# A two-layer attention and MLP trunk: another order of instructions, compressed scores inside a longer run, and an MLP without row factors

## The chip, the cores and the metric

The kernel runs on one core of a Trainium2 chip. The metric is the device time of one execution in microseconds. Engines are named as the profile names them: TensorE (PE, its weight loads PEld), VectorE (DVE), ScalarE (ACT), GpSimd (POOL) and SyncE (SP), whose queue issues the DMA transfers.

## What is computed

256 tokens of width 1024 pass through two layers. Each layer is a hybrid attention with a post-norm, and a squared-ReLU MLP of width 4096 with a post-norm, both around a residual:

```python
for l in range(DEPTH):
    h = _rms_norm(x, g_pre_mix[l])
    parts = jnp.split(h @ w_in[l], split_at, axis=-1)
    ...
    o_nsa = _nsa_mixer(...)      # 8 heads, 2 key heads: compressed, selected and window branch, gated
    o_fox = _fox_mixer(...)      # 8 heads, causal softmax with cumulative forget gates
    mix = jnp.concatenate([o_nsa, o_fox], axis=-1) @ w_out[l]
    x = x + _rms_norm(mix, g_post_mix[l])
    h = _rms_norm(x, g_pre_mlp[l])
    y = jnp.square(jax.nn.relu(h @ w_up[l])) @ w_down[l]
    x = x + _rms_norm(y, g_post_mlp[l])
```

`_rms_norm` divides by the root of the mean square plus 1e-6 and multiplies by a gain. In the compressed branch, keys and values of 32 tokens at a stride of 16 are flattened, pass a small two-layer network with gelu, and give 15 compressed keys and values for each key head. Queries are scored against them, the softmax of these scores (`pc`) weighs the compressed values, and it would also choose blocks of 64 tokens; as there are only four blocks and sixteen may be chosen, all of them are.

## The kernel before, in words

**Precision.** The large products are made from operands split in two parts of the type fp32r. For each chunk of weights ScalarE copies a rounded part `whi`, VectorE subtracts it to get `wlo` (`Weights.get`), and TensorE makes three products, hi·hi, lo·hi and hi·lo (`mm3`). The smaller products of attention, and the transposes, work on float32 operands directly. The tokens lie in two tiles of 128 (`NT`, index `t`).

**Stages.** For each layer: products of the normalised input with `w_in` in chunks (`in_chunk`; "c3", "c4" and so on are named groups of this filling work), attention, the output projection with `w_out`, norm and residual (`sandwich`), then `up` and `down` of the MLP in eight parts, norm and residual again. At the end of layer 0, `sandwich` makes the transposed input `xT` of layer 1, and layer 1's first products of `w_in` follow.

**What sets the order.** No instruction is issued where its line stands. The code runs against a `Recorder`, which notes every operation with its tiles, and `emit` issues them at line 392, the line that the profile shows for every instruction. Between the two stands a planner:

- `schedule` is a list scheduler. It keeps a time for each engine, and lets each engine take the ready operation with the lowest rank, as far as buffers are free. TensorE's rank is the recorded place (`key`), with the filling products in a lane of their own that runs at 0.9 of the main line's pace (`LANE`). A change of tile size on TensorE costs it `RETILE`, 145 ns.
- `order` runs it once with the recorded places, then calls `deadlines`, which works back from TensorE's order to a due time for each operation of the other engines, and runs `schedule` again with these due times as ranks, `PASSES` times. The last round counts.
- `_cost` and `_latency` give the planner's durations and delays. For TensorE, an fp32r product is taken as the larger of 107 ns and 3 + n/2.4 ns, a float32 product as the larger of 214 and n/0.6, transposes as 56 and 107 ns.
- `with nc.stretch()` binds several TensorE operations together, so that nothing gets between them.

So the planner's times decide what each of the five queues holds and in which order, and the chip then runs these queues with their semaphores.

**The places that the change touches.**

- *Compressed scores.* `hidden_part` makes the first product of the small network for keys ("k") and values ("v"): a stretch of 16 products on narrow tiles (`tile_position`, 32 columns of the array each, four side by side), named `o<-w,kst...` in the trace. `compressed_scores` scores the queries against the compressed keys (`kbd`) in a stretch of its own of four such products, `s<-qT,kbd`, and copies the result to `csT`. `compressed_exp` transposes it, adds the mask and takes the exponential; `compressed_scale` divides and makes `pcs`; `compressed_T` transposes it to `pcT`. `hidden_T` and `hidden_gelu` finish the values' network, `compressed_v` and `compressed_vT` give the block values `vbig`.
- *The attention loop.* A loop over 24 score tiles (16 of the sparse heads, 8 of the forgetting heads) calls for each `scores`, one step later `scale`, two steps later `probs_T` (three transposes of the softmax `pr`), and three steps later, for every second pair of heads, `pv` (a stretch of products on 64-wide tiles, `o<-pr...,v...`). Between them `fill(1)` puts in products of the next weights. The table `side` says beside which step each part of the compressed branch stands.
- *Block values.* After `pv` of sparse heads, one product of `vbig` and `pcT` adds the compressed branch to the same sum `o`. Its flags close the sum (`stop=True`). Then `o_evac` copies `o` to `oT`, split in two parts by ScalarE and VectorE.
- *Row factors of the MLP.* The input of the MLP is not divided by its root mean square. Because relu and square are homogeneous, the output only wants the factor r² per row. `row_factors` works out r, r² and r⁴ for each token tile, and `sandwich` takes them: `times` multiplies the sum by r² (a per-row scalar) and the gain in one `scalar_tensor_tensor`, and `rsqrt_sum` works out the root of r⁴·sum + eps.

Of the kernel before, what the change touches and what calls it, by code (L numbers as in the profile page):

```python
# [170 lines left out]
class Recorder:  # L171
# [103 lines left out]
    def order(self):  # L275

        for op in self.ops:
            op.rank = op.key
        out = self.schedule()
        for _ in range(PASSES):  # L280
            self.deadlines(out)
            out = self.schedule()
        return out

    def schedule(self):
# [41 lines left out]
        while events:  # L327
# [5 lines left out]
            for e, ops in waiting.items():  # L333
                while busy[e] <= t:
# [21 lines left out]
                    if e == "sync":  # L356
                        busy[e] = t + 450
                        bus = max(bus, t + 1150) + best.cost
                        best.end = bus + 900
                    else:  # L360
                        busy[e] = best.end = t + best.cost
                        if e == "tensor" and best.tile != tiled:
                            tiled = best.tile
                            busy[e] = best.end = best.end + RETILE
                    count += 1
# [55 lines left out]


def _cost(op, views):

# [5 lines left out]
    if op.engine == "tensor":  # L430
        if op.name == "stretch":

            return sum(x[1][0].ix.size / (2.4 if x[1][1].dtype == F32R else 0.6) + 20
                       for x in op.args[2]) / (P // min(op.tile))
        if op.name == "transpose":
            return 56.0 if op.args[1].dtype == F32R else 107.0
        if op.args[1].dtype == F32R:
            return max(107.0, 3 + n / 2.4)
        return max(214.0, n / 0.6)
    if op.engine == "vector":  # L440
# [63 lines left out]
def trunk(nc, A, consts_in, out, sbp, pp):  # L504
# [144 lines left out]

    def rsqrt_sum(a, b, factor=None):  # L650


        w = small([P, 6], "rsqrt", 6)
        c, d, h, y, t, r = (w[:, i:i + 1] for i in range(6))
        f = 1.0 if factor is None else factor
        nc.vector.tensor_scalar(c, a, f, EPS, op0=OP.mult, op1=OP.add)
        nc.vector.tensor_scalar(d, c, -0.5, None, op0=OP.mult)
        if factor is None:
            h = -0.5
        else:  # L660
            nc.vector.tensor_scalar(h, factor, -0.5, None, op0=OP.mult)
# [7 lines left out]
    def rstd_of_x(t, tag):  # L669
# [4 lines left out]
        return rsqrt_sum(ssq[:, 0:1], ssq[:, 1:2])  # L674

# [21 lines left out]

    def sandwich(t, acc, g_post, pre=None, xT=None, r4=None, r2=None, store=None):

# [4 lines left out]
        def times(name, n, gain):  # L704
            y = tokt(name)
            if r2 is None:
                nc.vector.tensor_mul(y, acc[n], gain[:, half(n)])
            else:
                nc.vector.scalar_tensor_tensor(y, acc[n], r2, gain[:, half(n)], op0=OP.mult, op1=OP.mult)
            return y  # L710

        for n in range(2):
# [4 lines left out]
            if n == 0 and not pre:  # L717
                m[0] = times("m", 0, g_post)
        r = rsqrt_sum(sq[:, 0:1], sq[:, 1:2], r4)
        if not pre:  # L720
# [54 lines left out]
    for l in range(DEPTH):  # L775
# [105 lines left out]
        def hidden_part(s, q):  # L881
            if q == 0:
                T["w1"] = []
            T["w1"].append(weight(l, "w1" + s, q))
            if q == 3:
                T["hid"] = psum("o")
                with nc.stretch():
                    for i in range(16):
                        c = i % 4
                        nc.tensor.matmul(T["hid"][32 * c:32 * c + 32, :256],  # L890
                                         kst[s][:, i, :, :].rearrange("p g n -> p (g n)"), T["w1"][i // 4][:, c, :],
                                         start=i < 4, stop=i >= 12, tile_position=(0, 32 * c))
                T["hs" + s] = tile([P, 256], F32, name="hs", tag="cum")
                nc.vector.tensor_copy(T["hs" + s], T["hid"][:, :256])
# [323 lines left out]

        def pv(o, pairs, last):


            with nc.stretch():
                for q, terms in enumerate(pairs):
                    for i, (pT, V, cols) in enumerate(terms):
                        for kb in range(2):
                            for par in range(2):
                                h = slice(par * HD, par * HD + HD)
                                c = cols[par]
                                if kb == 0:
                                    nc.tensor.matmul(o[h, q * S:q * S + S], V[0][:, c:c + HD], pT[par][:, 0:S],  # L1230
                                                     start=q == 0 and i == 0, stop=False, skip_group_check=True)
                                else:
                                    nc.tensor.matmul(o[h, q * S + P:q * S + S], V[1][:, c:c + HD], pT[par][:, S:S + P],
                                                     start=False, stop=last and i == len(terms) - 1,
                                                     skip_group_check=True)
# [10 lines left out]
        if first:  # L1246
            for n, _ in enumerate(in_chunk(0, evac0)):
                if n == 11:
# [4 lines left out]
                    for t in range(NT):  # L1253
                        r_mix[t] = rstd_of_x(t, "rm")
        else:

            for n, _ in enumerate(in_chunk(0, evac0, by_token=True)):
                if n == 6:
                    urgent(carry)
                    next(carry)  # L1260
                    for t in range(NT):
                        r_mix[t] = rstd_of_x(t, "rm")
        row_scales()
# [35 lines left out]
        for t in range(NT):  # L1299
# [14 lines left out]
        for i in range(len(flat) + 4):  # L1314
# [62 lines left out]
        r2s, r4s = [], []  # L1377
# [79 lines left out]
        for fc in range(8):  # L1457
# [25 lines left out]
            steps = [sandwich(t, [ys[t, 0], ys[t, 1]], g_post2, pre, xT, r4s[t], r2s[t],  # L1483
                              out[0].rearrange("(t p) d -> t p d", p=P)[t] if last_l else None) for t in range(NT)]
# [59 lines left out]
```

## Time and profile before

| what | value |
|---|---|
| time, median of 3 runs | 626.17 us (625.88 to 626.36) |
| the profiled execution's own time | 626.18 us |
| its span in the trace | 624.4 us |
| granted clock of TensorE | 0.998 |
| bytes moved | 115.70 MB, 185 GB/s |

Busy shares in 40 slices of 15.6 us, in tenths (9 is 90% or more):

```profile
PE   9999999999999999999999999999999999999995
DVE  6878999989986557566698899997997666566544
ACT  7757777577665455555566657764776555455432
DMA  8987446218766556654346883422396566556001
```

The first ten slices are layer 0's attention, the next ten its MLP; the twenty after them are the same for layer 1. TensorE is nearly always busy. VectorE is close to full in attention (slices 3 to 8, and 22 to 28) and half free in the MLPs; DMA is full only at the very start. In the rows that follow, a tile's name stands for all its buffers, `a<-b,c` is an output and its inputs, and since every instruction has line L392, groups are told apart by these names.

### The profile page before, as it was taken

The page shows a single profiled execution, that of the slowest core. Times are in us where ns is not written, and L with a number is a line of the kernel's source. Part 1 is how long each engine was busy: PE and PEld are TensorE (multiplying, and loading weights), DVE is VectorE, ACT ScalarE, POOL GpSimd, SP SyncE. Part 2 cuts the span into 40 slices and gives each one's busy share as a digit, 9 for nine tenths or more (in the row PEclk, how much of TensorE's full clock was granted, in tenths as well). Part 3 has the DMA queues.
Part 4 walks back from the last instruction along what each step waited for, and adds up shares of the span by engine and source line. Part 5 has one row for each costly group of instructions (what it writes and reads, how often), then busy time and mean ns, then how long its engine had stood idle before and what let it go on. Part 6 is the DMA issues. An engine that isn't in the chain of part 4 may idle for free.

```text
span 624.4 us, 9952 instructions
## 1 busy us (share of the span) xinstructions
PE 615.1 (99%) x3572; PEld 517.5 (83%) x3572; DVE 481.0 (77%) x1077; ACT 378.4 (61%) x736; POOL 0.2 (0%) x4
## 2 busy tenths in 40 slices
PE   9999999999999999999999999999999999999995
PEld 6988986788888888888888989778888888888884
DVE  6878999989986557566698899997997666566544
ACT  7757777577665455555566657764776555455432
POOL 0000000000000000000000000000000000000000
PEclk9999999999999999999999999999999999999999
DMA  8987446218766556654346883422396566556001
GB/s 322 403 341 257 150 153 199 88 56 318 266 192 203 194 175 201 198 180 136 102 156 218 303 290 118 164 81 90 105 318 204 183 186 209 180 189 193 22 1 68
DMA packets 33601, 115.70 MB, mean 185 GB/s; under 512 B 3984, under 2 KB 4112, under 8 KB 33552
## 3 DMA queue, kind: packets, MB, share of 16 engines
q1 hardware_dynamic: 33552, 115.07, 55.2%
q8 instruction: 28, 0.46, 0.3%
q14 instruction: 21, 0.17, 0.1%
HBM read 114.00 MB, written 1.05 MB: 184 GB/s over the span
## 4 chain that ended last, share of the span: by engine, by line
PE 91%; DVE 4%; DMA 2%; ACT 1%; issue 1%; DVEq 0%; SPq 0%
PE s L392 34%; PE acc L392 28%; PE x L392 24%; PE o L392 6%; DVE pr L392 2%; DMA wraw<-in_w_in_dram 1%; DVE wlo L392 1%; DMA first<-in_first_dram 1%; ACT whi L392 1%; ACT rl L392 0%; DVE cum L392 0%; DVE prT L392 0%; DVE st L392 0%; DVE prX L392 0%; ACT xT L392 0%
## 5 line engine op out<-in xcount | busy, mean ns | idle before, releaser
L392 DVE TENSOR_TENSOR wlo<-wraw,whi 128x1024 fp32r<-128x1024 f32 (+1 forms) x188 | 224.9, 1202 | 86.3 <-ACT whi L392 85.7
L392 ACT ACTIVATE whi<-wraw 128x1024 fp32r<-128x1024 f32 (+1 forms) x188 | 195.5, 1044 | 134.0 <-PE acc L392 70.3
L392 PE MATMUL s<-xT,whi 128*128 128x512 f32 x448 | 112.0, 392 | 0.0
L392 PEld LDWEIGHTS s<-xT,whi 128*128 128x128 f32 x448 | 81.4, 189 | 15.2
L392 PE MATMUL acc<-whi,aT 128*128 128x512 f32 x256 | 88.6, 390 | 0.0
L392 PE MATMUL x<-whi,aT 128*128 128x512 f32 x256 | 88.4, 390 | 0.0
L392 PEld LDWEIGHTS s<-xT,wlo 128*128 128x128 f32 x448 | 61.1, 190 | 4.4
L392 PE MATMUL s<-xT,wlo 128*128 128x256 f32 x448 | 62.5, 282 | 0.0
L392 PEld LDWEIGHTS acc<-whi,aT 128*128 128x128 f32 x256 | 48.0, 188 | 9.9
L392 PEld LDWEIGHTS x<-whi,aT 128*128 128x128 f32 x256 | 48.1, 188 | 9.6
L392 ACT ACTIVATE pr<-pr,st 128x256 f32<-128x256 f32 (+1 forms) x96 | 42.9, 450 | 15.6 <-DVE st L392 14.3
L392 PE MATMUL x<-wlo,aT 128*128 128x512 f32 x128 | 50.0, 390 | 0.0
L392 PE MATMUL acc<-wlo,aT 128*128 128x512 f32 x128 | 49.9, 390 | 0.0
L392 PE MATMUL acc<-xT,whi 128*128 128x256 f32 x256 | 48.8, 286 | 0.0
L392 PEld LDWEIGHTS acc<-xT,whi 128*128 128x128 f32 x256 | 40.4, 190 | 2.2 <-issue 1.2
L392 PE MATMUL x<-whi,xT 128*128 128x512 f32 x112 | 36.8, 400 | 0.4 <-ACT xT L392 0.3
L392 PE MATMUL acc<-xT,wlo 128*128 128x256 f32 x128 | 36.4, 285 | 0.0
L392 PE MATMUL acc<-whi,xT 128*128 128x512 f32 (+1 forms) x128 | 36.0, 352 | 0.0
L392 ACT ACTIVATE rl<-h 128x512 f32<-128x512 f32 x28 | 17.6, 629 | 18.2 <-DVE h L392 18.2
L392 PEld LDWEIGHTS acc<-wlo,aT 128*128 128x128 f32 x128 | 24.0, 188 | 5.0
L392 PEld LDWEIGHTS x<-wlo,aT 128*128 128x128 f32 x128 | 24.1, 188 | 4.5
L392 ACT ACTIVATE rl<-x 128x512 f32<-128x512 f32 x24 | 14.7, 612 | 21.6 <-PE x L392 16.6
(231 smaller groups left out, 974.7 us busy)
## 6 DMA issues: line engine op xcount, KB each, us to landing
wraw<-in_w_up_dram SPq DMA_DIRECT2D x64, 512.0 KB, 3.8
wraw<-in_w_down_dram SPq DMA_DIRECT2D x64, 512.0 KB, 3.6
wraw<-in_w_in_dram SPq DMA_DIRECT2D x36, 512.0 KB, 4.7
wraw<-in_w_out_dram SPq DMA_DIRECT2D x16, 512.0 KB, 6.2
w<-in_cmp_w_k_dram SPq DMA_DIRECT2D x8, 512.0 KB, 5.5
w<-in_cmp_w_v_dram SPq DMA_DIRECT2D x8, 512.0 KB, 5.8
first<-in_first_dram SPq DMA_DIRECT2D x7, 384.0 KB, 6.3
wraw<-in_w_in_dram SPq DMA_DIRECT2D x8, 288.0 KB, 4.2
```

Source lines behind the costliest of these rows:

```text
L392: getattr(getattr(self.nc, op.engine), name)(*[real(v) for v in args], **{k: real(v) for k, v in kw.items()})
```

## The change

It does four things.

1. **The planner.** `PASSES` goes from 1 to 4, and of all rounds the one with the earliest planned end is taken instead of the last. The planner's TensorE durations are replaced by others, taken from measurements (`_product`), and the cost of a change of tile size by 90 ns for leaving the full tile and 200 ns for the others.
2. **Compressed scores.** They are issued inside `hidden_part`'s stretch for the values, as its last group. The copy to `csT` moves to `compressed_exp`. The table `side` shifts: the filling "c3" at step 0, the values' `hidden_T` at step 2 and `hidden_gelu` at step 3 (steps 4 and 5 before).
3. **Block values first.** The product of `vbig` opens the sum `o`, and `pv` follows and closes it.
4. **The MLP without row factor.** The post-norm of the MLP is taken of the undivided sum, with eps·(ms + eps)² per row in place of eps, which is the same value. So `row_factors` makes one number per row in two instructions, `rsqrt_sum` loses its factor, and `times` is a plain `tensor_mul`.

```diff
-PASSES = 1
+PASSES = 4
...
-RETILE = 145
+ENTER, LEAVE = 90, 200
...
-        out = self.schedule()
+        out = best = self.schedule()
+        least = max(op.end for op in out)
         for _ in range(PASSES):
             self.deadlines(out)
             out = self.schedule()
-        return out
+            ends = max(op.end for op in out)
+            if ends < least:
+                best, least = out, ends
+        return best
...
+def _product(name, args, side):
+
+    n = int(np.prod(args[0].shape[1:]))
+    rounded = args[1].dtype == F32R
+    if name == "transpose":
+        return 85.0 if rounded else 109.0
+    if side > 1:
+        return n / 2.4 + 20 if rounded else n / 0.6 + (60 if n >= 256 else 11)
+    return max(118.0, n / 2.4 + (14 if n > 256 else 13)) if rounded else max(220.0, n / 0.6 + 7)
...
-    def rsqrt_sum(a, b, factor=None):
+    def rsqrt_sum(a, b, eps=EPS):
...
-        nc.scalar.activation(y, b, AF.Ln, bias=c, scale=f)
+        nc.scalar.activation(y, b, AF.Ln, bias=c)
         nc.scalar.activation(y, y, AF.Exp, scale=-0.5)
-        nc.vector.tensor_scalar(t, b, h, d, op0=OP.mult, op1=OP.add)
+        nc.vector.tensor_scalar(t, b, -0.5, d, op0=OP.mult, op1=OP.add)
...
             y = tokt(name)
-            if r2 is None:
-                nc.vector.tensor_mul(y, acc[n], gain[:, half(n)])
-            else:
-                nc.vector.scalar_tensor_tensor(y, acc[n], r2, gain[:, half(n)], op0=OP.mult, op1=OP.mult)
+            nc.vector.tensor_mul(y, acc[n], gain[:, half(n)])
             return y
...
+                    if s == "v":
+                        compressed_scores()
...
         def compressed_scores():
-            ps = psum("s")
-            with nc.stretch():
-              for p in range(4):
+            T["cps"] = ps = psum("s")
+            for p in range(4):
...
+        def compressed_exp():
             T["csT"] = small([P, S], "cs", 1)
-            nc.scalar.activation(T["csT"], ps[:, :S], AF.Copy)
-
-        def compressed_exp():
+            nc.scalar.activation(T["csT"], T["cps"][:, :S], AF.Copy)
...
-        side = {0: compressed_scores, 1: compressed_exp, 2: compressed_scale, 3: compressed_T,
-                4: lambda: (fill_to("c3"), hidden_T("v")), 5: lambda: hidden_gelu("v"),
+        side = {0: lambda: fill_to("c3"), 1: compressed_exp, 2: lambda: (compressed_scale(), hidden_T("v")),
+                3: lambda: (compressed_T(), hidden_gelu("v")),
...
                     o = psum("o")
+                    if br:
+                        nc.tensor.matmul(o, T["vbig"][:, pair // 2], T["pcT"][pair // 2], start=True, stop=False,
+                                         skip_group_check=True)
                     cols = lambda q: [(q // 2) * HD] * 2 if br else [2 * q * HD, 2 * q * HD + HD]
...
-                    if br:
-                        nc.tensor.matmul(o, T["vbig"][:, pair // 2], T["pcT"][pair // 2], start=False, stop=True,
-                                         skip_group_check=True)
...
         def row_factors():
+
             for t in range(NT):
-                r = rstd_of_x(t, "rp")
-                for tag, rs in (("r2", r2s), ("r4", r4s)):
-                    x = small([P, 1], tag, 4)
-                    nc.vector.tensor_mul(x, r, r)
-                    rs.append(x)
-                    r = x
+                a, b = squares_of_x(t, "rp")
+                x = small([P, 2], "epsr", 4)
+                nc.vector.scalar_tensor_tensor(x[:, 0:1], a, EPS, b, op0=OP.add, op1=OP.add)
+                nc.vector.scalar_tensor_tensor(x[:, 1:2], x[:, 0:1], EPS, x[:, 0:1], op0=OP.mult, op1=OP.mult)
+                epss.append(x[:, 1:2])
```

More of the change, by code (lines that the diff above doesn't have):

```diff
@@ L362, in schedule @@
                         if e == "tensor" and best.tile != tiled:
+                            busy[e] = best.end = best.end + (tiled == (P, P)) * ENTER + (tiled != (P, P)) * LEAVE
                             tiled = best.tile
-                            busy[e] = best.end = best.end + RETILE
                     count += 1
@@ L431, in _cost @@
         if op.name == "stretch":
[L433 to L439, printed above, removed]
+            side = P // min(op.tile)
+            return sum(_product(*x[:2], side) for x in op.args[2][::side])
+        return _product(op.name, op.args, 1)
     if op.engine == "vector":
@@ L648, in split @@
         nc.vector.tensor_sub(dst[1], src, dst[0].bitcast(F32))
-    def rsqrt_sum(a, b, factor=None):
[L653 to L656, printed above, removed]
-        nc.vector.tensor_scalar(d, c, -0.5, None, op0=OP.mult)
-        if factor is None:
-            h = -0.5
-        else:
-            nc.vector.tensor_scalar(h, factor, -0.5, None, op0=OP.mult)
-        nc.scalar.activation(y, b, AF.Ln, bias=c, scale=f)
+    def rsqrt_sum(a, b, eps=EPS):
+        w = small([P, 5], "rsqrt", 6)
+        c, d, y, t, r = (w[:, i:i + 1] for i in range(5))
+        nc.vector.tensor_scalar(c, a, eps, None, op0=OP.add)
+        nc.vector.tensor_scalar(d, c, -0.5, None, op0=OP.mult)
+        nc.scalar.activation(y, b, AF.Ln, bias=c)
         nc.scalar.activation(y, y, AF.Exp, scale=-0.5)
-        nc.vector.tensor_scalar(t, b, h, d, op0=OP.mult, op1=OP.add)
+        nc.vector.tensor_scalar(t, b, -0.5, d, op0=OP.mult, op1=OP.add)
         nc.vector.scalar_tensor_tensor(t, y, t, y, op0=OP.mult, op1=OP.mult)
@@ L667, in rsqrt_sum, with squares_of_x @@
         return r
-    def rstd_of_x(t, tag):
+    def squares_of_x(t, tag):
         ssq = small([P, 2], tag + "s")
@@ L673, in rstd_of_x @@
             nc.scalar.activation(junk, X[t][:, half(n)], AF.Square, scale=1.0 / 32.0, accum_out=ssq[:, n:n + 1])
-        return rsqrt_sum(ssq[:, 0:1], ssq[:, 1:2])
+        return ssq[:, 0:1], ssq[:, 1:2]
     def new_xT():
@@ L696, in pre_gain, with sandwich @@
         return g_next, xo
-    def sandwich(t, acc, g_post, pre=None, xT=None, r4=None, r2=None, store=None):
+    def sandwich(t, acc, g_post, pre=None, xT=None, eps=EPS, store=None):
         sq = small([P, 2], "sq")
@@ L718, in sandwich @@
                 m[0] = times("m", 0, g_post)
-        r = rsqrt_sum(sq[:, 0:1], sq[:, 1:2], r4)
+        r = rsqrt_sum(sq[:, 0:1], sq[:, 1:2], eps)
         if not pre:
@@ L1217, in probs_T, with pv @@
             return pT
-        def pv(o, pairs, last):
+        def pv(o, pairs, alone):
             with nc.stretch():
@@ L1230, in pv @@
                                     nc.tensor.matmul(o[h, q * S:q * S + S], V[0][:, c:c + HD], pT[par][:, 0:S],
-                                                     start=q == 0 and i == 0, stop=False, skip_group_check=True)
+                                                     start=alone and q == 0 and i == 0, stop=False, skip_group_check=True)
                                 else:
                                     nc.tensor.matmul(o[h, q * S + P:q * S + S], V[1][:, c:c + HD], pT[par][:, S:S + P],
-                                                     start=False, stop=last and i == len(terms) - 1,
+                                                     start=False, stop=i == len(terms) - 1,
                                                      skip_group_check=True)
@@ L1253, in trunk @@
                     for t in range(NT):
-                        r_mix[t] = rstd_of_x(t, "rm")
+                        r_mix[t] = rsqrt_sum(*squares_of_x(t, "rm"))
         else:
@@ L1261, in trunk @@
                     for t in range(NT):
-                        r_mix[t] = rstd_of_x(t, "rm")
+                        r_mix[t] = rsqrt_sum(*squares_of_x(t, "rm"))
         row_scales()
@@ L1376, in trunk @@
             params = load_params(l + 1)
-        r2s, r4s = [], []
+        epss = []
         def row_factors():
             for t in range(NT):
-                r = rstd_of_x(t, "rp")
-                for tag, rs in (("r2", r2s), ("r4", r4s)):
-                    x = small([P, 1], tag, 4)
-                    nc.vector.tensor_mul(x, r, r)
-                    rs.append(x)
-                    r = x
+                a, b = squares_of_x(t, "rp")
[3 more added lines that the diff above has]
+                epss.append(x[:, 1:2])
         def up(fc, then=None):
@@ L1482, in trunk @@
             ws = [None] * 4
-            steps = [sandwich(t, [ys[t, 0], ys[t, 1]], g_post2, pre, xT, r4s[t], r2s[t],
+            steps = [sandwich(t, [ys[t, 0], ys[t, 1]], g_post2, pre, xT, epss[t],
                               out[0].rearrange("(t p) d -> t p d", p=P)[t] if last_l else None) for t in range(NT)]
```

1 line of the change is left out of this document (removed).

## The prediction

> **What bounds the kernel now.** I read the shares of the page first, then the chain of waits, then what TensorE waited for, then busy time by stage, then single places on the timeline.
>
> ```profile
> span 624.4 us, 9952 instructions
> PE 615.1 (99%) x3572; PEld 517.5 (83%) x3572; DVE 481.0 (77%) x1077; ACT 378.4 (61%) x736; POOL 0.2 (0%) x4
> PE 91%; DVE 4%; DMA 2%; ACT 1%; issue 1%; DVEq 0%; SPq 0%
> ```
>
> The first line is the span, the second the busy time of each engine, the third the chain that ended last. TensorE (PE) is busy for 615.1 of 624.4 us and holds 91% of the chain. The time can therefore fall in three ways only: fewer or cheaper products, less time lost where TensorE changes its kind of work, or fewer waits. What TensorE waited for is a short list (total, times, longest):
>
> ```profile
> PE o L392 <- DVE warm L392: 1.2, 1, 1.2
> PE s L392 <- DVE kW L392: 0.5, 1, 0.5
> PE x L392 <- ACT oT L392: 0.4, 1, 0.4
> PE x L392 <- ACT xT L392: 0.3, 1, 0.3
> PE x L392 <- DVE oT L392: 0.2, 1, 0.2
> ```
>
> The first line is the start of the program and stays. The other four are 1.4 us in all, 0.2% of the span, and they lie in the attention stages and at the layers' junction. The stages say the same (window: length, PE busy, PEld, DVE, ACT, POOL, clock, DMA share, GB/s):
>
> ```profile
> 60.00:95.00 35.00, 35.00 (x248) 30.68 (x247) 34.04 (x131) 25.46 (x72) 0.00 (x0) 1.00 0.49 171
> 95.00:125.00 30.00, 29.64 (x204) 21.71 (x203) 28.81 (x92) 18.46 (x54) 0.00 (x0) 1.00 0.46 142
> 157.00:305.00 148.00, 148.00 (x743) 126.01 (x742) 99.02 (x132) 81.15 (x117) 0.00 (x0) 1.00 0.60 192
> 320.00:340.00 20.00, 19.52 (x116) 16.85 (x115) 18.22 (x51) 15.81 (x35) 0.00 (x0) 1.00 0.72 237
> 370.00:400.00 30.00, 30.00 (x215) 26.19 (x214) 28.97 (x107) 21.47 (x61) 0.00 (x0) 1.00 0.46 155
> 400.00:432.00 32.00, 31.78 (x217) 23.51 (x216) 28.24 (x99) 21.21 (x63) 0.00 (x0) 1.00 0.34 113
> ```
>
> In the MLP (157 to 305 us) TensorE has no idle moment and VectorE (DVE) has 49 us to spare: what the change takes from VectorE there is hidden under products and worth nothing. In attention VectorE is almost full: 34.04 of 35 us and 28.97 of 30. TensorE doesn't wait there, but only because the order fits. This is where a new order can lose.
>
> **The change part by part.** Both kernels issue the same 3344 products and transposes, so nothing is gained from work; only order, neighbours and waits differ. The instruction orders of the two builds give the counts below, the trace the prices. Two prices are used throughout: a 512-column product, and a transpose.
>
> ```profile
> 311.07 5.23 PE o L392 x23
> ```
>
> 23 products in 5.23 us of the chain are 0.227 us each. The transposes are read off the next but one fence.
>
> *Compressed scores in the run of the values' products.* Now they are a run of their own, with a narrow tile (128\*32) among full ones:
>
> ```profile
> 57.70 0.28 PE L392 MATMUL acc<-xT,wlo 128*128 128x256 f32 x1
> 57.82 0.28 PE L392 MATMUL acc<-xT,whi 128*128 128x256 f32 x1
> 58.03 0.64 PE L392 MATMUL s<-qT,kbd 128*32 128x256 f32 x8
> 58.60 0.38 PE L392 MATMUL acc<-xT,whi 128*128 128x256 f32 x1
> 58.82 0.28 PE L392 MATMUL acc<-xT,wlo 128*128 128x256 f32 x1
> ```
>
> Read the starts: 57.70 to 57.82 is an ordinary step, 0.12. The step into the run takes 0.21 (0.09 too long), the run 0.57, the step after it 0.22 (0.10 too long): 0.76 us in all. As a further group in a run that exists anyway it costs what a group costs there:
>
> ```profile
> 53.27 1.93 PE L392 MATMUL o<-w,kstv 128*32 128x256 f32 x32
> 55.14 0.50 PE L392 MATMUL x<-kx,qS 128*128 128x512 f32 x1
> ```
>
> 32 records take 55.14 − 53.27 = 1.87, 8 took 0.57, both with one beginning and end; so 24 records cost 1.30, and 8 cost 0.43. The gain is 0.76 − 0.43 = 0.33 per layer, **0.66 us**. The Trainium skill (TensorEngine Tiling (Array Packing), Key Properties) says that a change of tiling mode drains TensorE, and TensorE: Matmul & The Clock Gate, Part 2, step 4, gives that drain as some 128 cycles at 2.4 GHz, so by my estimate from these pages 0.05 us a change: four changes fewer would be worth 0.2 us, where the rows above give 0.66. The trace has 0.09 and 0.10 for the two changes and a longer run beside them, so the rows decide.
>
> *Block values first.* In the kernel before, the product vbig comes behind three transposes that follow the values' products, so the attention output o is ready late:
>
> ```profile
> 105.41 0.55 PE L392 MATMUL s<-cst,pr 128*128 128x128 f32 x3
> 105.71 0.48 PE L392 MATMUL o<-pcT,vbig 128*128 128x512 f32 x1
> 106.03 0.49 PE L392 MATMUL s<-cst,pr 128*128 128x128 f32 x3
> 106.23 0.60 ACT L392 ACTIVATE oT<-o 128x512 fp32r<-128x512 f32 x1 [1.06 <-PE o L392]
> 106.89 0.50 PE L392 MATMUL x<-whi,oT 128*128 128x512 f32 x1 [0.36 <-ACT oT L392]
> ```
>
> Three transposes step 0.30 (105.41 to 105.71). From 106.03 TensorE is through at 106.33, and starts the output projection at 106.89: 0.56 lost to the copy oT. With vbig ahead of the values, o ends before 105.41 instead of near 106.1, some 0.65 earlier; oT can end 0.65 earlier, at about 106.2, which is before 106.33. The **0.56 us** goes. Next in line is then the product's own weights, long split. Its twin in layer 1:
>
> ```profile
> 402.02 0.67 PE L392 MATMUL s<-cst,pr 128*128 128x128 f32 x3
> 402.91 0.50 PE L392 MATMUL x<-whi,oT 128*128 128x512 f32 x1 [0.22 <-DVE oT L392]
> ```
>
> 402.91 − 402.32 = **0.59 us**, for the same reason.
>
> *The new order (more rounds, measured durations).* At the junction TensorE waits twice. First for the next layer's input:
>
> ```profile
> 316.81 0.60 PE L392 MATMUL s<-cst,mg 128*128 128x128 f32 x4
> 317.66 0.50 PE L392 MATMUL x<-whi,xT 128*128 128x512 f32 x1 [0.25 <-ACT xT L392]
> ```
>
> Four transposes are 0.40, so 317.21 could have been the start: **0.45 us** lost. In the changed order products of the next layer's first chunk lie among the transposes: five of them and four transposes stand between the last transpose of the first half and the product that needs it, 5 × 0.227 + 4 × 0.10 = 1.5 us of cover, against a copy of the size of oT's 0.60; and a VectorE split that stood ahead of these transposes stands behind them. Then for the rotated window key:
>
> ```profile
> 335.00 0.62 PE L392 MATMUL x<-whi,xT 128*128 128x512 f32 x2
> 335.75 0.21 DVE L392 TENSOR_TENSOR kW<-rope,rope 128x64 f32<-128x64 f32 x1
> 336.11 0.30 PE L392 MATMUL s<-cst,kW 128*128 128x128 f32 x1 [0.48 <-DVE kW L392]
> 336.16 0.48 PE L392 MATMUL x<-wlo,xT 128*128 128x512 f32 x1
> ```
>
> Two products from 335.00 end at 335.45, the transpose starts at 336.11: **0.66 us**. In the changed order one split (1.22, last fence of this part) and one scaling of vW (some 0.3) that VectorE did before kW come after it, so kW is some 1.5 us earlier; the transpose itself moves ahead of four products, 0.9 us. What is left, 0.6, is just the wait: between 0 and 0.66 goes, and I take **0.5 us**, near the upper end.
>
> *MLP without the row factor.* It leaves VectorE 24 instructions fewer, all on one column, and ScalarE 8, and turns 12 scalar_tensor_tensor into plain multiplications. All are under products, but for the end of the program:
>
> ```profile
> 618.51 0.75 DVE L392 SCALAR_TENSOR_TENSOR m<-acc,r,gains 128x512 f32<-128x512 f32 x1 [1.65 <-ACT rl L392]
> 619.18 0.27 DVE L392 TENSOR_SCALAR rsqrt<-sq,rsqrt 128x1 f32<-128x1 f32 x1
> L392 DVE TENSOR_TENSOR m<-acc,gains 128x512 f32<-128x512 f32 x4 | 2.6, 685 | 0.0
> L392 DVE TENSOR_TENSOR wlo<-wraw,whi 128x1024 fp32r<-128x1024 f32 x180 | 218.9, 1222 | 85.8 <-ACT whi L392 85.3
> ```
>
> There m (0.75) becomes such a multiplication (0.685), and the step behind it loses an operand from memory: between 0 and 0.12, I take 0.06. **0.13 us**.
>
> Gains: 0.66 + 0.56 + 0.59 + 0.45 + 0.5 + 0.13 = 2.89 us.
>
> *What the order costs.* (a) In layer 1 two runs of the forgetting heads' scores no longer stand directly ahead of a run of values: transposes come between, two changes of tile more. Between 0 and 0.19 each (the compressed run's 0.09 + 0.10); I take 0.15, so 0.3. (b) The row-scale transpose of layer 1 moves 16 products of 288 columns earlier, while VectorE's chain to it moves by less. No row shows it; from 0, if the chain has slack, to 0.8, a little over the longest stall above (0.66); I take 0.4, between. (c) Layer 0 asks three more splits (3 × 1.222 = 3.67 us) of VectorE before the compressed probabilities and before the first oT. I count 0.3 for two just-late transposes there (0 to 3.67, see the second rival). (d) SyncE (SP) issues the first chunk's weights two or three places earlier and the four x tiles later, and in the MLP two w_up loads ahead of others; ScalarE's squares of x then wait with a split of weights queued behind them: 0 to 0.5, I take 0.1, near the lower end, since the bytes ahead of the last of them stay the same. Together 1.1 us.
>
> Net: 2.89 − 1.1 = 1.79 us. The profiled execution took 626.18 us (span 624.4 and 1.78 around it), within 0.01 of the median of 626.17, so the forecast is 626.18 − 1.79 = **624.4 us**.
>
> **The rivals.**
>
> 1. *The waits move and don't vanish.* Only what is counted stays: 0.66 for the runs and 0.13 at the end, less 0.3 for the two lost neighbours, gives 0.5 us: **625.7 us**. For it: the waits are 0.2 to 0.6 us each, and an order worked out with durations that are a few per cent off makes new ones of that size. Against it: the five removed ones have named causes, and each cause moves by 0.65 us or more.
> 2. *VectorE becomes the bound in attention* (the other side). In 60 to 95 us it has 0.96 us idle, in 370 to 400 us 1.03. If the three added splits (3.67 us) aren't absorbed by its idle time before 60 us, its chain to the compressed probabilities is late by up to 3.67 − 0.96 = 2.7 us, and TensorE, which has only ordered work there, waits for it. It decides once the splits come more than 0.96 us into that chain. With the counted gains of rival 1: 626.18 − 0.5 + 2.7 = 628.4 us at most, half of it 627.0; I take **627.7 us**. Against it: the splits are earlier work, not more work, and TensorE can use what they prepare.
> 3. *The change doesn't do what it says*: more rounds leave the order where it was. The instruction orders exclude this for the order; for vbig, whose own inputs could be late, the rival gives back 0.56 + 0.59 alone: 624.4 + 1.15 = **625.5 us**.
>
> **How the numbers follow.** Chances: forecast 0.52, rival 1 0.17, rival 3 0.08, rival 2 0.23. The forecast's own spread is the unknown costs: all at their low ends would be 626.18 − 3.05 (with all of kW's 0.66) = 623.1; with (a) to (d) high but VectorE keeping up, and nothing from kW, 2.39 − (0.38 + 0.8 + 0.3 + 0.5) = 0.4, so 625.8. The range goes from 623.1 up to 627.6, which leaves out half of rival 2. A measurement of this kernel can tell some 0.2%, 1.25 us, from no change. Faster (under 624.9) is most of the forecast and a little of rivals 1 and 3: 0.50. Same (624.9 to 627.4) is the rest of these and some of rival 2: 0.32. Slower 0.18.
>
> **What would show it.** Right: 128\*32 runs two fewer, each merged run about 0.43 us longer; oT, xT and kW gone from the list of what TensorE waited for; VectorE about 4 us less busy, all of it without effect on the MLP's 148 us. The step (b) shows as a wait for rsqrt near 325 us, (c) as waits for cs, pcs or pr between 58 and 75 us. Wrong: waits of TensorE of more than 1.5 us in all beside the start, or a longer MLP stage.

## The result, and the profile after

The changed kernel takes 629.25 us (median of 6 runs, 627.81 to 631.1) against 626.04 us (6 runs, 625.86 to 626.37): ratio 1.0053, 95% interval 1.0036 to 1.0071. It is slower by 0.5%, where 624.4 us was forecast, and the range ended at 627.6. Its runs also spread over 3.3 us, those of the kernel before over 0.5. The profiled execution took 628.81 us with a span of 627.0. The page, with the lines shown of before:

```profile
span 627.0 us, 9924 instructions
PE 616.6 (98%) x3572; PEld 518.2 (83%) x3572; DVE 479.8 (77%) x1053; ACT 375.4 (60%) x728; POOL 0.2 (0%) x4
PE 86%; DVE 8%; DMA 3%; issue 1%; ACT 1%; DVEq 0%
```

TensorE's share of the chain fell from 91 to 86%, VectorE's and DMA's rose from 4 to 8 and from 2 to 3%. What TensorE waited for (total, times, longest):

```profile
PE s L397 <- DVE q_rot L397: 1.3, 2, 0.7
PE o L397 <- DVE warm L397: 1.2, 1, 1.2
PE x L397 <- DVE kW L397: 0.9, 1, 0.9
PE s L397 <- DVE kW L397: 0.2, 1, 0.2
```

The waits for oT and xT of before are gone, as forecast. What stands under kW has grown from 0.5 to 1.1 us, and q_rot is new. Both lie where layer 1 makes its keys and queries. Beside the start the list is 2.4 us, 1.4 before: the prediction's sign of being wrong (more than 1.5) has come. Busy time in 318 to 356 us, before and after (length, PE, PEld, DVE, ACT, POOL, clock, DMA share, GB/s):

```profile
318.00:356.00 38.00, 37.52 (x264) 32.53 (x262) 33.94 (x87) 26.11 (x52) 0.00 (x0) 1.00 0.72 242
```

```profile
318.00:356.00 38.00, 35.64 (x244) 30.41 (x243) 33.64 (x85) 25.99 (x50) 0.00 (x0) 1.00 0.75 248
```

TensorE is idle for 2.36 us there, 0.48 before: of the 2.6 us by which the two profiled executions differ, 1.9 are lost in these 38 us. VectorE isn't full (33.64 of 38). DMA is busy for three quarters of the window. (It isn't full at the very start alone: its row of slices ahead of the prediction has an 8 or 9 also in slices 10, 23, 24 and 30, and slice 23 begins at 343 us.)

Another 0.5 us is lost before: the last product of layer 0's MLP (`acc<-whi,aT`) starts at 311.20 us, 310.68 before. In that layer the compressed run (0.33) and the wait for oT (0.56) are won, so some 1.4 us go elsewhere in it. No row of TensorE's waits shows them. A product's record lasts 0.39 us where its step to the next is 0.23, so a delay shorter than the difference counts as busy; TensorE's busy time grew by 1.5 us with as many instructions. What delays it there was not tested.

Now one of these waits on the timeline of the changed kernel, all engines:

```profile
325.70 0.33 SPq L397 DMA_DIRECT2D wraw<-in_w_in_dram  x1
...
331.55 1.06 ACT L397 ACTIVATE whi<-wraw 128x1024 fp32r<-128x1024 f32 x1 [1.42 <-DMA wraw<-in_w_in_dram]
...
332.51 0.46 ACT L397 ACTIVATE kW<-acc,rsqrt 128x256 f32<-128x256 f32 x1
...
333.00 0.43 DVE L397 TENSOR_TENSOR rope<-kW,cst 128x64 f32<-128x64 f32 x3 [1.12 <-ACT kW L397]
...
333.61 0.34 DVE L397 TENSOR_SCALAR vS<-x,rsqrt 128x128 f32<-128x128 f32 x1
...
334.10 0.47 PE L397 MATMUL x<-whi,xT 128*128 128x512 f32 x1 [0.89 <-DVE kW L397]
```

Read it from the last line up. TensorE waits for VectorE. By the names, its product writes the tile x that vS still has to read; the bracket names kW, which ran just behind vS. VectorE is late because it was idle for 1.12 us before it could rotate kW, the step ahead of vS. ScalarE had not made kW, because the copy of a weight chunk (whi) stood ahead of it in its queue, and that copy stood still for 1.42 us, until its transfer had landed, some 5.8 us after SyncE issued it at 325.70 (the order of loads and copies gives the pair). The table of waits names VectorE; the cause is a transfer, two queues away. The second q_rot wait has the same shape, with a split of that late copy (wlo) ahead of q_rot on VectorE too:

```profile
345.11 9.68 SPq L397 DMA_DIRECT2D wraw<-in_w_in_dram  x7
...
350.38 1.06 ACT L397 ACTIVATE whi<-wraw 128x1024 fp32r<-128x1024 f32 x1 [1.94 <-DMA wraw<-in_w_in_dram]
351.34 0.61 ACT L397 ACTIVATE q_rot<-q 128x512 fp32r<-128x512 f32 x1
...
351.47 1.23 DVE L397 TENSOR_TENSOR wlo<-wraw,whi 128x1024 fp32r<-128x1024 f32 x1 [0.91 <-ACT whi L397]
...
352.61 0.68 DVE L397 TENSOR_TENSOR q_rot<-q,q_rot 128x512 fp32r<-128x512 f32 x1
...
353.44 1.19 PE L397 MATMUL s<-identr,q_rot 128*128 128x128 f32 x12 [0.68 <-DVE q_rot L397]
```

In all, ScalarE's weight copies waited for w_in transfers (before, then after):

```profile
ACT whi L392 <- DMA wraw<-in_w_in_dram: 5.5, 8, 1.5
```

```profile
ACT whi L397 <- DMA wraw<-in_w_in_dram: 8.7, 9, 1.9
```

And the kernel before had such a place already. It is the one whose wait for kW the prediction quoted from TensorE's and VectorE's rows alone; these are ScalarE's, a moment earlier:

```profile
334.08 1.06 ACT L392 ACTIVATE whi<-wraw 128x1024 fp32r<-128x1024 f32 x1 [1.45 <-DMA wraw<-in_w_in_dram]
...
335.30 0.46 ACT L392 ACTIVATE kW<-acc,rsqrt 128x256 f32<-128x256 f32 x1
```

Two small gains came as forecast. The compressed scores now stand in the run: from the first of its products to the first ordinary one behind it are 59.27 − 56.97 = 2.30 us, against 1.87 for the run without them, so 0.43 for the group:

```profile
56.97 1.93 PE L397 MATMUL o<-w,kstv 128*32 128x256 f32 x32
58.72 0.61 PE L397 MATMUL s<-qT,kbd 128*32 128x256 f32 x8
59.27 0.38 PE L397 MATMUL acc<-xT,whi 128*128 128x256 f32 x1
```

And at the end, from m to the last step (x) it takes 622.62 − 621.26 = 1.36 us, against 620.00 − 618.51 = 1.49, which is 0.13 less:

```profile
621.26 0.69 DVE L397 TENSOR_TENSOR m<-acc,gains 128x512 f32<-128x512 f32 x1 [1.69 <-ACT rl L397]
...
622.62 1.41 DVE L397 SCALAR_TENSOR_TENSOR x<-m,rsqrt,x 128x512 f32<-128x512 f32 x2
```

```profile
620.00 1.41 DVE L392 SCALAR_TENSOR_TENSOR x<-m,rsqrt,x 128x512 f32<-128x512 f32 x2
```

### The profile page after: what moved, and what is told of

The parts are those of the page before. It is cut to its first block, busy times and chain, and to the rows that moved or that the text cites. A ratio compares the mean times of both kernels' runs of the same rounds, so it can differ in the third digit from the quotient of the medians.

```text
span 627.0 us, 9924 instructions
## 1 busy us (share of the span) xinstructions
PE 616.6 (98%) x3572; PEld 518.2 (83%) x3572; DVE 479.8 (77%) x1053; ACT 375.4 (60%) x728; POOL 0.2 (0%) x4
## 4 chain that ended last, share of the span: by engine, by line
PE 86%; DVE 8%; DMA 3%; issue 1%; ACT 1%; DVEq 0%
PE s L397 33%; PE acc L397 24%; PE x L397 23%; PE o L397 6%; DVE wlo L397 3%; DMA wraw<-in_w_in_dram 3%; DVE pr L397 2%; ACT whi L397 0%; DVE x L397 0%; DVE gz L397 0%; DVE m L397 0%; DVE rope L397 0%; DVE cum L397 0%; DVE q L397 0%; DVE q_rot L397 0%
## 5 line engine op out<-in xcount | busy, mean ns | idle before, releaser
L397 PE MATMUL acc<-xT,whi 128*128 128x256 f32 x256 | 50.2, 289 | 0.0
L397 PE MATMUL acc<-whi,xT 128*128 128x512 f32 (+1 forms) x128 | 38.0, 359 | 0.0
L397 DVE TENSOR_TENSOR h<-rl 128x512 f32<-128x512 f32 x28 | 19.4, 691 | 16.8 <-ACT rl L397 16.8
```

Of the source, the lines that this page charges most:

```text
L397: getattr(getattr(self.nc, op.engine), name)(*[real(v) for v in args], **{k: real(v) for k, v in kw.items()})
```

## The experiments

All ratios are to the kernel before, run beside each variant; each time is a median of 5 to 11 runs.

### First theory: one split moved, and with it the first load

The first theory was wrong. In the changed kernel the last split ahead of the junction's transposes stands behind them. It frees the buffer for layer 1's first w_in transfer, which SyncE issues at 318.67 us instead of 312.63. The theory: this makes all loads late. The rival: VectorE too full in attention, the second of the prediction. Swapping the split with the multiplication m that stood in its old place undoes just that:

```diff
+        name = lambda op: op.args[0].buf.name if op.engine == "vector" and isinstance((op.args or [0])[0], View) else ""
+        split = [op for op in best if name(op) == "wlo"][103]
+        late = [op for op in best[:best.index(split)] if name(op) == "m"][-1]
+        i = best.index(late)
+        best[best.index(split)] = late
+        best[i] = split
         return best
```

> The changed kernel, every queue as it is, but for one pair on VectorE: the last split before the junction's transposes changes places with the multiplication m that stands ahead of them. Late load: first w_in transfer of layer 1 near 313 us, the waits for vS and kW near 333 us (1.4 us in all) and perhaps those for q_rot near 348 and 352 us (1.6 us) go, up to 0.5 us is lost at the transposes, so 626.5 to 628.0. VectorE too full in attention: no change, 629.2, or 0.5 us more.

Measured: 629.29 us, ratio 1.0046 (1.0033 to 1.0059), no better than the changed kernel. The first load was issued at 312.29, so the edit did what it should; but the second one came at 322.47, as before the swap (322.59), and TensorE was idle in the window for as long as without it (first the window, then its waits, of which those for qS and mg are new):

```profile
318.00:356.00 38.00, 35.61 (x242) 30.35 (x240) 33.26 (x85) 25.40 (x50) 0.00 (x0) 1.00 0.68 230
```

```profile
PE x L403 <- DVE kW L403: 1.0, 1, 1.0
PE s L403 <- ACT qS L403: 0.7, 1, 0.7
PE s L403 <- DVE q_rot L403: 0.6, 1, 0.6
PE s L403 <- DVE mg L403: 0.6, 1, 0.6
```

The MLP without row factor, alone, moves the same split by itself:

> The kernel before with the MLP without row factor alone. The same split stands behind the transposes here too, though the planner's costs are the old ones. Late load: first w_in transfer of layer 1 near 318.5 us, 1 us or more lost between 325 and 355 us, 627 to 628.5 us. VectorE too full in attention: VectorE has less to do here, so no loss, 625.9 to 626.1 (0.13 us gained at the end).

Measured: 626.15 us, ratio 1.0001 (0.9993 to 1.0010). Its first load is issued at 318.73, and TensorE has no idle moment in the window:

```profile
318.00:356.00 38.00, 38.00 (x267) 33.53 (x266) 34.85 (x89) 27.15 (x52) 0.00 (x0) 1.00 0.77 252
```

So a late first load costs nothing in this kernel, and the theory falls twice. VectorE as rival did not predict these idle times either: they lie where it has 4 to 5 us to spare.

### The four parts alone

The planner's part alone (the durations, the costs of changes of tile, and the rounds):

> The kernel before with the first part of the change alone (rounds, best of them, measured durations). In its instruction order the last split of weights at the layers' junction stands behind the transposes of the normed output, as in the changed kernel. Late load (the split frees the buffer for the first w_in transfer of layer 1, so everything that ScalarE copies from there on is late): that transfer is issued near 318.5 us instead of 312.6, TensorE loses 1 us or more between 325 and 355 us, and the time is 627.5 to 629.5. VectorE too full in attention: slower by 2 to 3 us too, but lost between 58 and 125 and between 360 and 430 us. The order as forecast: 624.5 to 625.5.

Measured: 631.03 us, ratio 1.0077 (1.0063 to 1.0091), the worst of all, with 2.33 us of idle time in the same window:

```profile
318.00:356.00 38.00, 35.67 (x240) 30.36 (x239) 33.78 (x86) 25.23 (x49) 0.00 (x0) 1.00 0.72 241
```

That is 1.9 us more than before, of a loss of 4.9 between the two profiled executions. The last product of layer 0's MLP is late by 1.6 us already (312.24), and in layer 1's attention TensorE waits for VectorE's vrep (0.6 us). VectorE is busy for 34.71 of 35 us between 60 and 95 us and for 29.63 of 30 between 370 and 400, more than before: outside the window the prediction's second rival isn't excluded.

The rounds have no share in this. Built with four rounds and the old durations, every queue is the same as in the kernel before, and this variant has the same queues with one round as with four, since the round kept is the first. In the whole change it is not so: there the third round is kept (planned end 620.04 us, 620.13 after the first), and the whole change with one round was not timed. Without any of the planner's part, but with the three others:

> The changed kernel with the planner of before (one round, old durations, last round taken). The split stands behind the transposes here too. Late load: 627 to 629, first w_in transfer of layer 1 near 318.5 us. VectorE too full because of the new order: without that order nothing is lost, and the counted gains of the runs, of the block values and of the end are left: 624.5 to 625.5.

Measured: 628.99 us, ratio 1.0047 (1.0034 to 1.0059). This one has no idle time in that window at all:

```profile
318.00:356.00 38.00, 38.00 (x261) 33.09 (x260) 34.51 (x87) 26.46 (x51) 0.00 (x0) 1.00 0.74 244
```

It loses in other places (the norm after layer 0's attention, and the scores in layer 1): the last product of layer 0's MLP is late by 2.6 us (313.30). So the whole change's loss and this one's are not the same loss. Its list of TensorE's waits doesn't show it (1.2 us beside the start, less than before); the busy time does, 617.9 us against 615.1. The two remaining parts alone:

> The kernel before with the compressed scores in the run of the values' products and the shifted side table, and nothing else. Margin and transfers: the planner keeps its short durations, so 625.3 to 626.3 (0.66 us gained in runs, some of it lost again). Lucky order of before: 628 or above. If this part's own dependences cost what the variant without the new planner lost (2.8 us), it shows here: 628 to 629.

Measured: 627.57 us, ratio 1.0024 (1.0014 to 1.0033), above the 625.3 to 626.3 that were expected: the edit is the second part of the change, alone. It has the runs' gain (the merged run takes 2.30 us here too). The waits for oT stand as before, that for st is new, and beside the start the list is 2.0 us against 1.4, too little for what was lost:

```profile
PE x L392 <- ACT oT L392: 0.7, 2, 0.4
PE s L392 <- DVE kW L392: 0.6, 1, 0.6
PE s L392 <- DVE st L392: 0.3, 1, 0.3
```

> The kernel before with the product of the block values put ahead of the values' products, and nothing else. As forecast, the two waits for oT (0.56 and 0.59 us) go and nothing comes: 625.0 to 625.5. If each new plan loses something on the chip, whatever the part: 626.5 to 628.

Measured: 626.84 us, ratio 1.0010 (1.0001 to 1.0019). A miss of the forecast's clearest step, in the range that the expectation gave to "each new plan loses something". The wait for oT at 106 us is gone (one of 0.2 us for VectorE's part of oT is left in all), but TensorE waits at the norm, for the first half of the MLP's input. In the kernel before five products of `w_out` lie among and behind the norm's eight transposes; in this plan none do. Eight transposes from 130.61 would be through at 131.5 by 0.11 each; the product starts at 132.04, and another 0.3 us goes two products later, at the second half:

```profile
130.61 1.19 PE L392 MATMUL s<-cst,mg 128*128 128x128 f32 x8
131.40 0.59 ACT L392 ACTIVATE xT<-s 128x512 fp32r<-128x512 f32 x1
132.04 0.50 PE L392 MATMUL s<-whi,xT 128*128 128x512 f32 x1 [0.24 <-ACT xT L392]
```

### Second theory: weight copies that wait for transfers stand ahead of what TensorE wants

The planner takes a transfer of 512 KB as 1150 + 524288/360 + 900 ns = 3.5 us when the queue is free (the lines in `schedule` and `_cost`). The trace has 4.7 us as the median of the w_in loads of 512 KB before, and 5.6 in the changed kernel. A plan that believes 3.5 puts whi where it expects the transfer to be there; ScalarE's queue doesn't overtake, so an activation behind it waits as well.

Why did the kernel before get away with it? Its planner took a 512-column product as 3 + 512/2.4 = 216 ns, where the trace has 227. Its plan ends at 590.0 us, the span is 624.4: TensorE's work was planned some 5% short. On the chip TensorE runs that much behind its plan, and whatever another engine or a transfer does too late by a few us is covered. The measured durations take this cover away: the changed kernel's plan ends at 620.0 us, its span is 627.0. That is the theory; its test must be made at the copies, at the planned transfers, and at the cover.

*The copies.* TensorE's and SyncE's queues stay, three copies and two splits go behind what they blocked:

```diff
...
+        behind("scalar", "whi", 112, "kx", 1)
+        behind("scalar", "whi", 115, "q_tok", 2)
+        behind("vector", "wlo", 116, "q_rot", 1)
+        behind("scalar", "whi", 116, "q_rot", 1)
+        behind("vector", "wlo", 117, "q_rot", 1)
         return best
```

(`behind(engine, name, k, mark, nth)` takes the k-th operation that writes a tile of that name out of the order and puts it behind the nth following one that writes `mark`.)

> The changed kernel with its TensorE and SyncE queues as they are; in layer 1's input stage three copies of weights (whi) on ScalarE go behind the activations kx, q_tok and q_rot that they stand ahead of, and two splits on VectorE behind q_rot. Weight copies waiting for their transfers at the head of ScalarE's queue: the waits for kW and vS near 333 us and for q_rot near 348 and 352 us, 2.2 to 3.0 us in all, go, and the time is 626.2 to 627.2. VectorE too full: those waits stay, 629 or above. The kernel before simply has a lucky order, and any other loses somewhere: 628 to 630, new waits in other places.

Measured: 626.77 us, ratio 1.0013 (1.0004 to 1.0022): 2.5 of the 3.2 us come back. TensorE's waits, and the place at 333 us with ScalarE now in the other order:

```profile
PE o L412 <- DVE warm L412: 1.2, 1, 1.2
PE s L412 <- ACT qS L412: 0.3, 1, 0.3
PE s L412 <- DVE qS L412: 0.2, 1, 0.2
```

```profile
332.35 0.48 ACT L412 ACTIVATE kW<-acc,rsqrt 128x256 f32<-128x256 f32 x1
...
332.72 0.59 ACT L412 ACTIVATE kx<-s 128x512 fp32r<-128x512 f32 x1
333.20 1.06 ACT L412 ACTIVATE whi<-wraw 128x1024 fp32r<-128x1024 f32 x1
```

The copy starts at 333.20 without any wait, its transfer landed meanwhile, and no kW waits for it. No product, no transfer and no instruction was added or taken away. TensorE's idle time in the window falls from 2.36 to 0.39 us (37.61 of 38 busy). ScalarE's copies still wait for w_in for 5.1 us in all (8.7 without the edit), but no longer ahead of what TensorE wants. This is the cleanest of the tests, since it leaves TensorE's order alone; the next ones give a new plan for all engines.

*The planned transfers.* The changed kernel, every transfer planned 2.0 us later:

```diff
-LANDING = 2500.0
+LANDING = 4500.0
...
-                        best.end = bus + 900
+                        best.end = bus + 2900
```

> The changed kernel, whose planner expects each transfer 2.0 us later (2900 in place of 900 ns of delay, due times with 4500 in place of 2500), about what the trace shows of the w_in loads (5.6 us against a planned 3.5). Transfers later than planned: the new order has loads and copies early enough, TensorE's waits beside the start fall under 1 us, 624.5 to 627. Lucky order of before: 628 to 631. VectorE too full: 628 to 630, since its load is the same.

Measured: 625.40 us (624.82 to 625.78), ratio 0.9987 (0.9978 to 0.9996). The fastest of all, and faster than both kernels. Its waits are the start alone (warm and gcol, both before 6 us), and ScalarE's copies wait for w_in once (the first two lines are TensorE's, the third is ScalarE's):

```profile
PE o L397 <- DVE warm L397: 1.2, 1, 1.2
PE x L397 <- DVE gcol L397: 0.5, 1, 0.5
...
ACT whi L397 <- DMA wraw<-in_w_in_dram: 1.5, 1, 1.5
```

Its loads still take 5.4 us to land between 318 and 352 us (5.8 in the changed kernel): the transfers did not become faster, the plan became right about them. With half the dose (1.0 us):

> The changed kernel with half the dose, 1.0 us. Transfers later than planned: between the changed kernel (629.2) and the one with 2.0 us (625.4), 626 to 628, and a wait left where a weight copy stands ahead of an activation. If the 2.0 us only happened on a good order: anywhere from 625 to 631.

Measured: 625.93 us, ratio 0.9995 (0.9986 to 1.0004), just under the expected range. A wait for kW of 0.3 us is left, and the copies wait for 4.7 us in all, between 8.7 and 1.5. The dose shows in the cause as it should, but the time follows it less than evenly: most is gained with the first 1.0 us. On the planner's part alone, the worst kernel:

> The kernel before with the measured durations, and a planner that expects each transfer 2.0 us later. Transfers later than planned were the loss of the measured durations (631.0 us without the 2.0): 625.5 to 627.5. If the loss lay in the new costs of TensorE as such: 629.5 to 631.

Measured: 627.06 us, ratio 1.0012 (1.0003 to 1.0021), from 631.03. The same two numbers in the planner give back 4.0 us. The waits that are left (1.2 us beside the start) are for VectorE's st and vrep in attention. In the window TensorE has no idle moment:

```profile
318.00:356.00 38.00, 38.00 (x265) 33.32 (x264) 34.44 (x95) 26.07 (x53) 0.00 (x0) 1.00 0.70 237
```

*The cover.* The changed kernel with all planned TensorE durations taken times 0.94:

> The changed kernel with the planner's TensorE durations all 6% short, so that its plan ends near where that of the kernel before did and every other engine and transfer has those 6% as a margin on the chip. Margin lost with the measured durations: 624.5 to 627. Lucky order of before: 628 to 631.

Measured: 626.02 us (625.06 to 628.45), ratio 1.0003 (0.9994 to 1.0012). The copies still wait for w_in transfers (6.5 us in all), but TensorE is idle for 0.07 us in the window:

```profile
318.00:356.00 38.00, 37.93 (x266) 33.26 (x265) 34.87 (x94) 27.61 (x53) 0.00 (x0) 1.00 0.77 257
```

So here a wrong duration for one engine paid for a wrong duration of another resource. And the kernel before, whose plan has this cover already, with the 2.0 us:

> The kernel before with nothing but the 2.0 us. Its short TensorE durations are a margin already, so there is little to gain: 625.5 to 626.5. If the late transfers cost every plan the same: 624 or below. If any new plan loses: 627 to 630.

Measured: 627.28 us, ratio 1.0018 (1.0009 to 1.0026). It is slower by 1.1 us, not what was expected, but in the range that the expectation gave to "any new plan loses": the waits for oT stand as before, and small ones between 80 and 110 and from 380 to 420 us are new. What is shown by it: the 2.0 us are no gain in themselves. Taken with the two runs of the planned transfers, they undo the loss that comes with honest TensorE durations.

What stays open: the 0.7 us by which the variant with the copies behind is still over the kernel before, and why the plans with old durations lose 0.6 (block values), 1.1 (the 2.0 us alone), 1.5 (compressed scores) and 2.8 us (three parts together). The traces show in part where (small waits in scattered places, and time that counts as busy), but none of it was taken away by itself. Four of the five other plans made with the old durations are slower than the kernel before and none is faster, so the rival "the kernel before has a lucky order" survives outside layer 1's input stage.

## Why the prediction was wrong

- **The step that failed is the wait for kW under "the new order".** The prediction read it as VectorE's order ("one split and one scaling ... that VectorE did before kW come after it"), and gave a gain of 0.5 us. The runs showed 0.9 us at the same step of VectorE's chain, and 0.2 more at kW's own transpose. VectorE had been idle ahead of it: it waited for ScalarE's kW, that for whi, and that for a transfer. With three such copies put behind, 2.5 us came back. The bracket on ScalarE's row, 1.45 us for DMA, stood in the trace of before, and so did the 1% of the chain on w_in transfers. With this read, the question would have been when TensorE wants kW and q_rot, and when their transfers land, for which the brackets in the rows of the changed kernel show 0.6 to 0.9 us at each of three places.
- **A term mis-sized: (c), the cost of the new order in layer 0.** It was put at 0.3 us against gains of 0.89 there. The layer came out 0.5 us late, so 1.4 us were lost in it, of which the waits that (c) named show 0.14. The cause stays open.
- **No rival named a transfer.** The second rival ended near the measured time (627.7 against 629.25) by another mechanism, VectorE; its signs, waits for cs and pcs between 58 and 75 us, did not come in size. TensorE is late by 0.14 us ahead of pcs, and by nothing at cs.
- **"An order worked out with durations that are a few per cent off" was put down as a danger of the new plan.** It was the other way in layer 1's input stage: the old plan's errors were its safety, and putting them right took it away. The 0.94 bears this out (626.02 us, 0.07 us idle in the window), in one plan.
- **Right in mechanism and size:** compressed scores (0.43 us for the group, as worked out, so 0.33 saved per layer), the end of the program (0.13), the waits for oT and xT gone, nothing gained in the MLP (148.00 of 148 us busy before and after). The wait (b) for the row scales did not come. One sign did not come either: VectorE is 1.2 us less busy, not 4; the MLP without row factor alone gives 3.4.
- **Right, but worth nothing:** block values first. In the whole change the waits for oT went; done alone, the one in layer 0 went, and some 0.8 us came back at the next norm. The prediction asked what is next in line behind oT's wait, and looked one instruction ahead, not at the next place where TensorE meets another engine.
- The prediction's sum took the removed waits as won in full (kW's nearly) and added guesses for new ones (1.1 us). With waits of half a microsecond in a plan without slack, the sum of removed waits was an upper bound here, not a forecast.

## What to carry to other kernels

When a planner's costs are corrected, look for the ones that were not: an engine planned too short can be a hidden margin for everything that was never measured. Follow a wait of TensorE back through each queue until an instruction waits for something that isn't a queue; the releaser in the table is only the last link. And in an in-order queue, work that waits for a transfer belongs behind work whose operands are there.

## What the runs showed of the hardware

A load of 512 KB took 4.7 us (before) and 5.8 us (changed kernel), as medians, from issue to landing in the input stage of layer 1, while the core moved some 245 GB/s; in the best plan it was 5.4. The time varied from run to run by 3.3 us with the copies ahead (627.81 to 631.1), by 1.4 with three of them behind (626.3 to 627.68), by 1.0 where the plan knows the delay (624.82 to 625.78). Copies that wait are not enough for that: in the kernel before they wait for 5.5 us, and its 33 runs beside the last variants spread by 1.5. What varies was not measured.
